# Placing the down-weight sums of a two-layer decoder trunk at single products instead of behind whole pairs

## The chip, the cores and the metric

The kernel runs on one core of a Trainium2 chip. A core has a matrix engine (PE in the profile, with its weight loads as PEld), a vector engine (DVE), a scalar engine (ACT), a general engine (POOL), a queue engine that only issues transfers (SP), and 16 DMA engines that all queues share. The metric is the device time of one execution in microseconds; times given for a kernel are medians of several runs.

## The reference

The reference is a decoder trunk of two layers on a sequence of 512 positions with 1024 channels, in 32-bit floats. Layer 0 mixes tokens by causal pooling, layer 1 by causal differential attention; each is followed by a dense SwiGLU block of 2816 hidden channels. Only that block is touched here:

```
x = layernorm(ALPHA * x + mixer(x))
x = layernorm(ALPHA * x + (silu(x @ w_gate) * (x @ w_up)) @ w_down)
```

## The kernel before

Every 32-bit operand is held as two parts, a rounded high part and a low remainder, and a product is three matmuls (high by high, high by low, low by high). ACT makes the high part (a cast) and DVE the low part (a subtraction). Weights come from one DRAM tensor, `wall`, in rows of 128x1024.

**The gate and up products.** The function `ffn(layer, late)` is called once per layer, as `ffn(0, ...)` and `ffn(1, ...)`. The 22 hidden blocks of 128 are taken two at a time as eleven units, 0 to 10, in the order `f0 f1 f2 p2 f3 p3 p4 p5 p6 p7 p8 p9 p10`: a unit `f` is half a pair made plainly, a unit `p` a whole pair made by a fast matrix scheme with seven products instead of eight. Pairs 4 to 10 make the seven in the order P1, Q5, P6, Q3, P7, P2, Q4 (`GATE`; `strassen(k)`). Each product needs a weight piece of its own, `g_N` with parts `g_Nh` and `g_Nl`; the pieces of pair 5 are g_29 to g_35, of pair 9 g_57 to g_63, of pair 10 g_64 to g_70, in the order of the products. P1, P6, P7 and Q4 add up in the PSUM bank A, Q5 and Q3 in the bank C, P2 in the bank B. Between products partial results are copied out: P1 from A to B by ACT (L1000), Q5 from C to `hid` by ACT (L1002), P6 from A to `hid` by ACT (L1004), Q3 and P7 by DVE (L1009, L1011). A product that adds to a bank must wait until the bank's last copy is done: so Q3 waits for L1002, P6 for L1000, P7 for L1004. `ahead(...)` has the pieces of the next products prepared up to six products ahead (L697 sums of weight rows on DVE, L700 casts on ACT, L703 remainders on DVE). The pieces go through six buffers in turn.

**The sums of down weights.** The product with `w_down` comes later (the down stage) and uses the same fast scheme, so it needs sums of blocks of `w_down`. They are made while the gate and up products run, in eleven steps, sum 0 to sum 10, in order:

- `load_terms(k)`: POOL issues two loads of four blocks (L808) and then one transfer that adds blocks to the first two (L809, an accumulating DMA that waits for the loads). For even k below 10 the place is a set of rows of `hid` that is not yet in use, for odd k and for 10 the tile `b`, of which there is one.
- `sum_terms(k)`, first half: two DVE additions of 128x512 (L814, L815). Second half: ACT issues two DMAs (L819) that write the four results to `tsum` in DRAM, and POOL issues `load_terms(k + 2)`. Since `load_terms(10)` reuses `b`, it is issued behind sum 9, and its loads wait until both writes of sum 9 have landed.

`weight_sums()` does the first half at once and leaves the second half to `catch_up()`, which is called behind the `ahead` of every product. So the writes of a sum stand one product behind its additions in ACT's order.

The program is written out by hand in this order, and each engine runs its own instructions in order. An instruction that waits holds what stands behind it on its engine, a DMA issue on ACT included. In the printed lists of an engine's rows the names read out<-in.

Of the kernel before, what the change touches and what calls it, by code (L numbers as in the profile page):

```python
# [49 lines left out]
EARLY = (1, 0)  # L50
PRE = SPLIT[:2]
SUMS = {1: (2, 1), 2: (2, 1)}
SUMMED = {"f0": 0, "p2": 0, "p4": 2, "p10": 0}
EAGER = 6


# [20 lines left out]
def trunk(ctx, tc, x, wall, pscale, lam_p, subln, table, lng, lnb, band, first, onehot, out):  # L77
# [6 lines left out]
    def bank(name):  # L84
        return ps.tile([P, 512], F32, tag="bank", name=name)
# [481 lines left out]
    def ffn(layer, late):  # L567
# [7 lines left out]
        with tc.tile_pool(name=f"ffn{layer}", bufs=1) as fp:  # L575
# [115 lines left out]
            def do_step(at=0):  # L691
                kind, j = steps.pop(at)
                c, pair = chunks[j]
                refill()
                t = raws[c]
                if kind == "sum":
                    tt(t, raws[pair[0]], raws[pair[1]], op=ALU.add)  # L697
                elif kind == "cast":
                    halves[j] = weight_pair(f"g{layer}_{j}")
                    nc.scalar.copy(halves[j][0], t)  # L700
                else:
                    h, l = halves[j]
                    tt(l, t, h.bitcast(F32), op=ALU.subtract)  # L703
                    finished.add(j)
                for d in set((c,) + pair):
                    if uses[d] == (kind, j):
                        raws.pop(d)
                        held[0] -= 1
# [103 lines left out]
            def sum_terms(k):  # L812
                t = terms.pop(k)
                tt(t[:, 1, 1], t[:, 0, 0], t[:, 1, 1], op=ALU.add)  # L814
                tt(t[:, 1, 0], t[:, 1, 1], t[:, 1, 0], op=ALU.add)  # L815
                yield
                dst = tsum[:, k // 2, :, term_slice(k)].rearrange("(j r) p t -> p j r t", j=2)
                for j in range(2):
                    nc.scalar.dma_start(out=dst[:, j], in_=t[:, j])  # L819
                if k + 2 < HALF - 1:  # L820
                    load_terms(k + 2)
                if k == HALF - 2:
                    load_terms(HALF - 1)
# [4 lines left out]
            def weight_sums():  # L828
                g = sum_terms(summed_rows[0])
                summed_rows[0] += 1  # L830
                next(g)
                behind.append(g)
# [4 lines left out]
            def catch_up():  # L837
                for g in list(behind):
                    if next(g, g) is g:
                        behind.remove(g)  # L840
# [49 lines left out]
            def both(t):  # L890
                return t.rearrange("p (f t) -> p f t", f=2)

            def half_product(acc, j, left, start, stop, high_first=False):
                h, l = halves[j]
                xh, xl = left
                terms_of = ((h, xh), (h, xl), (l, xh))
                places = [(f, kk) for f in range(2) for kk in range(4)]
                if high_first:
                    todo = [(f, kk, w, x) for w, x in terms_of for f, kk in places]
                else:  # L900
                    todo = [(f, kk, w, x) for f, kk in places for w, x in terms_of]
                for i, (f, kk, w, x) in enumerate(todo):
                    c = slice((4 * f + kk) * P, (4 * f + kk + 1) * P)
                    nc.tensor.matmul(  # L904
                        acc[:, f * 256 : (f + 1) * 256], w[:, c], x[:, kk, :],
                        start=start and i == 0,
                        stop=stop and i == len(todo) - 1,
                        skip_group_check=True,
                    )
# [70 lines left out]
            def strassen(k):  # L980
                names = {"P1": "A", "P6": "A", "P7": "A", "Q4": "A", "Q5": "C", "Q3": "C", "P2": "B"}
                begun = k in PRE
                banks = {"A": pre_a[k] if begun else bank(f"A{layer}_{k}"), "C": bank(f"C{layer}_{k}")}
                banks["B"] = bankB
                rows = hid[:, k : k + HALF + 1 : HALF, :]
                first, second = rows[:, :, :256], rows[:, :, 256:]

                def tile_of(i):
                    return keep.tile([P, S], F32, tag="y", name=f"sg{layer}_{k}_{i}", bufs=2)

                for p in BEGUN if begun else GATE:
                    acc = banks[names[p]]
                    j = number[k, GATE.index(p), "pair"]
                    half_product(
                        acc, j, lefts[p], p in ("P1", "Q5"), p in ("Q4", "Q3", "P2"),
                        k == PRE[0] and p == "Q4",
                    )
                    acc = both(acc)
                    if p == "P1":
                        nc.scalar.copy(both(bankB), acc)  # L1000
                    elif p == "Q5":
                        nc.scalar.copy(second, acc)  # L1002
                    elif p == "P6":
                        nc.scalar.copy(first, acc)  # L1004
                    elif p == "Q3":
                        if begun:
                            g0 = pre_g[k]
                            nc.scalar.activation(g0, g0, AF.Silu)
                        tt(first, acc, first, op=ALU.subtract)  # L1009
                    elif p == "P7":  # L1010
                        tt(second, second, acc, op=ALU.subtract)  # L1011
                    elif p == "P2":
                        g0 = tile_of(0)
                    else:
                        g1 = tile_of(1)
                        nc.scalar.activation(both(g1), acc, AF.Silu)  # L1016
                    if k == PRE[0] and p == "Q5":
                        while steps[0] != ("low", number[k, 6, "pair"]):
                            do_step()
                    else:  # L1020
                        ahead(j + lookahead(k, p))
                    if not (k == PRE[0] and p == "Q5"):
                        catch_up()
                    if p == "P2":
                        nc.scalar.activation(both(g0), acc, AF.Silu)
                    elif p == "Q4":
                        tt(first, both(g0), first, op=ALU.mult)  # L1027
                        tt(second, both(g1), second, op=ALU.mult)
                sum_hidden(k)

            for kind, i in units(layer):
                (plain if kind == "f" else strassen)(i)
                unit = f"{kind}{i}"
                for _ in range(SUMMED.get(unit, 1)):
                    weight_sums()
                if unit in AFFINE:
                    affine(n - 1, *AFFINE[unit])
# [634 lines left out]
```

## Time and profile before

| what | us |
|---|---|
| median of 3 runs (lowest, highest) | 934.05 (932.45, 934.33) |
| the profiled execution: its own time | 930.78 |
| the profiled execution: span from first to last instruction | 929.0 |
| PE busy in that span | 916.7 |
| DVE busy | 804.6 |
| ACT busy | 530.2 |
| POOL busy | 110.5 |

The granted clock of PE was 0.997 in the mean. Times inside the execution are microseconds from the start of the span. The gate and up stage of layer 0 with its pairs 4 to 10 lies at about 120 to 262, that of layer 1 at about 675 to 816. A row of a timeline reads: start, duration, engine, line, operation, out<-in, shape, count, and in brackets how long the engine sat idle just before it and what ended that. ACTq and POOLq are the sequencers of ACT and POOL. In the list of DMA issues the last number of a row is the time in microseconds from the issue to the landing.

### The profile page before, as it was taken

Reading aid. Unit: us, or ns where it says so; the run is one execution under the profiler, and the core shown is the slowest. Engines: PE = TensorE matmul, PEld = TensorE weight load, DVE = VectorE, ACT = ScalarE, POOL = GpSimd, SP = SyncE. Lnnn points to the kernel's source line nnn. Section 1 sums busy time; section 2 is a strip of 40 time slices with the busy share of each in tenths; the row PEclk is TensorE's granted clock in tenths of the full one; section 3 lists DMA queues with packets and bytes.
Section 4 is the critical chain, followed back from the end, with each engine's and each line's share of the span. In section 5 each row is a group of like instructions: output and inputs, shape, how many; then the busy total and the mean of one; then the engine's idle time right before and its main releaser. Section 6 shows DMA issues by size and latency. Waiting matters only on the chain. (4 is left out here: it accounts for less than half of the span.)

```text
span 929.0 us, 15065 instructions
## 1 busy us (share of the span) xinstructions
PE 916.7 (99%) x5806; PEld 826.2 (89%) x5806; DVE 804.6 (87%) x1163; ACT 530.2 (57%) x841; POOL 110.5 (12%) x129
## 2 busy tenths in 40 slices
PE   9999999999999999999999999999999999999996
PEld 8999899999988888888888888989999999988885
DVE  8997798999889997868989786877898998989988
ACT  6773354444555557776878864843454444655551
POOL 4121112110000001201111100201111110000001
PEclk9999999999999999999999999999999999999998
DMA  8497888985756578876665522467888985745563
GB/s 230 168 269 222 272 257 270 288 258 183 236 174 202 195 241 235 224 194 166 153 153 155 155 92 77 142 199 242 275 254 264 286 278 181 227 171 204 193 205 102
DMA packets 72518, 192.50 MB, mean 207 GB/s; under 512 B 14548, under 2 KB 14804, under 8 KB 72446
## 3 DMA queue, kind: packets, MB, share of 16 engines
q1 hardware_dynamic: 44572, 121.36, 39.1%
q0 software_dynamic: 15712, 46.93, 22.1%
q10 hardware_dynamic: 12162, 23.25, 6.7%
q8 instruction: 45, 0.74, 0.3%
q14 instruction: 27, 0.22, 0.1%
HBM read 166.33 MB, written 25.19 MB: 206 GB/s over the span
## 5 line engine op out<-in xcount | busy, mean ns | idle before, releaser
L697 DVE TENSOR_TENSOR raw<-raw,raw 128x1024 f32<-128x1024 f32 x72 | 87.8, 1221 | 6.8 <-DMA raw<-in_wall 5.8
L156 DVE TENSOR_TENSOR xs<-hid,xs 128x512 fp32r<-128x512 f32 x84 | 53.4, 637 | 0.0
L155 ACT CAST xs<-hid 128x512 fp32r<-128x512 f32 x84 | 48.5, 580 | 0.4 <-DVE hid L1027 0.4
L1303 ACT ACTIVATE p<-p,mn 128x128 f32<-128x128 f32 (+3 forms) x64 | 35.2, 552 | 14.1 <-DVE mn L1298 14.1
L808 POOL DMA_DIRECT2D b<-in_wall x24 | 18.9, 875 | 132.8 <-DMA tsum<-b 52.6
L1002 ACT COPY hid<-C 128x512 f32<-128x512 f32 x18 | 10.6, 588 | 33.9 <-PE C L904 16.0
L1298 DVE CUSTOM_DVE_ANT_0 p<-s,bias 128x128 f32<-128x128 f32 (+3 forms) x64 | 28.0, 485 | 1.1 <-PE s L1283 1.1
L808 POOL DMA_DIRECT2D hid<-in_wall x20 | 15.0, 753 | 112.3 <-DVE hid L814 35.8
L1009 DVE TENSOR_TENSOR hid<-C,hid 128x512 f32<-128x512 f32 x18 | 12.4, 689 | 16.5 <-PE C L904 13.2
L231 POOL TENSOR_TENSOR rs<-rs,mhalf 128x1 f32<-128x1 f32 x16 | 12.8, 802 | 103.2 <-DVE rs L230 96.2
L282 ACT ACTIVATE y<-pt,bT,gT 128x128 f32<-128x128 f32 x40 | 15.0, 456 | 15.9 <-PE pt L268 15.8
L1016 ACT ACTIVATE sg<-A 128x512 f32<-128x512 f32 x18 | 10.7, 596 | 22.7 <-PE A L904 22.7
L222 DVE BATCH_NORM_STATS2 st<-res 128x6 f32<-128x512 f32 x32 | 22.2, 694 | 1.1
L1004 ACT COPY hid<-A 128x512 f32<-128x512 f32 x18 | 10.6, 587 | 21.4 <-PE A L904 21.4
L809 POOL DMA_DIRECT2D b<-in_wall x12 | 14.8, 1230 | 60.5 <-DMA b<-in_wall 60.5
L1317 DVE SCALAR_TENSOR_TENSOR p<-p,sm,p 128x128 f32<-128x128 f32 (+3 forms) x32 | 17.6, 551 | 1.1
L1011 DVE TENSOR_TENSOR hid<-hid,A 128x512 f32<-128x512 f32 x18 | 12.3, 682 | 7.2 <-PE A L904 7.0
L762 ACT CAST xs<-hid 128x1024 fp32r<-128x1024 f32 x8 | 8.4, 1051 | 14.3 <-DVE hid L771 8.7
L261 DVE TENSOR_TENSOR res<-res,gb 128x512 f32<-128x512 f32 (+1 forms) x20 | 16.0, 799 | 0.7
L156 POOL TENSOR_TENSOR sql<-sq,sqh 128x512 fp32r<-128x512 f32 x7 | 9.3, 1324 | 60.5 <-ACT sqh L155 60.5
L260 DVE TENSOR_TENSOR res<-res,gb 128x512 f32<-128x512 f32 (+1 forms) x20 | 15.8, 792 | 0.0
L809 POOL DMA_DIRECT2D hid<-in_wall x10 | 12.4, 1241 | 28.7 <-DMA hid<-in_wall 28.6
(1218 smaller groups left out, 3561.7 us busy)
## 6 DMA issues: line engine op xcount, KB each, us to landing
raw<-in_wall SPq DMA_DIRECT2D x130, 512.0 KB, 5.7
r<-tsum SPq DMA_DIRECT2D x40, 512.0 KB, 3.7
b<-in_wall POOLq DMA_DIRECT2D x36, 512.0 KB, 6.1
hid<-in_wall POOLq DMA_DIRECT2D x30, 512.0 KB, 6.6
r<-in_wall SPq DMA_DIRECT2D x30, 512.0 KB, 4.1
tsum<-b ACTq DMA_DIRECT2D x24, 512.0 KB, 5.5
tsum<-hid ACTq DMA_DIRECT2D x20, 512.0 KB, 5.9
tall<-in_wall POOLq DMA_DIRECT2D x3, 1024.0 KB, 12.4
```

Of the source, the lines that this page charges most:

```text
L155: nc.scalar.copy(dst_h, src)
L156: (low or nc.vector).tensor_tensor(dst_l, src, dst_h.bitcast(F32), op=ALU.subtract)
L222: nc.vector.bn_stats(stats[n, s][:, d, :], res[:, s, d * 512 : (d + 1) * 512])
L260: nc.vector.tensor_tensor(z, z, gb[:, 0, c], op=ALU.mult)
L261: nc.vector.tensor_tensor(z, z, gb[:, 1, c], op=ALU.add)
L282: nc.scalar.activation(y[:, k, :], pt[:, k * P : (k + 1) * P], AF.Identity, bias=bT[:, n, kk : kk + 1], scale=gT[:, n, kk : kk + 1],)
L697: tt(t, raws[pair[0]], raws[pair[1]], op=ALU.add)
L808: nc.gpsimd.dma_start(out=t[:, j], in_=src[:, j])
L809: nc.gpsimd.dma_start(out=t[:, 0], in_=src[:, :, 1], accum_op=ALU.add)
L1298: nc.vector.tensor_tensor_reduce(out=p, in0=accs[c], in1=biases[h][:, w - 1 :: -1] if w < S else biases[h][:, ::-1], op0=ALU.add, op1=ALU. ...
L1303: nc.scalar.activation(p, p, AF.Exp, bias=mn[:, q, c : c + 1], scale=-1.0, accum_out=sm[:, q, c : c + 1],)
L1317: nc.vector.scalar_tensor_tensor(p0[:, r], p0[:, r], sm[:, q, 0:1], p1[:, r], op0=ALU.mult, op1=ALU.add)
```

## The change

`SUMMED` was a table that said how many sums are made behind a unit (one where nothing was said); it becomes a list of places. A place is the end of a unit, as before, or a product within a pair, behind the `catch_up()` of that product.

```diff
-SUMMED = {"f0": 0, "p2": 0, "p4": 2, "p10": 0}
+SUMMED = ("f1", "f2", "f3", "p3", "p4", "p5P2", "p6P7", "p7P7", "p8P6", "p9Q5", "p9")
...
                     if not (k == PRE[0] and p == "Q5"):
                         catch_up()
+                    if f"p{k}{p}" in SUMMED:
+                        weight_sums()
...
                 unit = f"{kind}{i}"
-                for _ in range(SUMMED.get(unit, 1)):
+                if unit in SUMMED:
                     weight_sums()
```

| sum | 0 | 1 | 2 | 3 | 4 | 5 | 6 | 7 | 8 | 9 | 10 |
|---|---|---|---|---|---|---|---|---|---|---|---|
| before: behind | f1 | f2 | f3 | p3 | p4 | p4 | p5 | p6 | p7 | p8 | p9 |
| now: behind | f1 | f2 | f3 | p3 | p4 | P2 of p5 | P7 of p6 | P7 of p7 | P6 of p8 | Q5 of p9 | p9 |

The instructions are the same in kind and number on every engine; the lines behind the second edit move down by two (L1025, L1027 and L1028 before are L1027, L1029 and L1030 now), the lines 697 to 1016 that are named here stay. Both layers change alike. Where the order moves, in layer 0:

ACT at the front of pair 5, before (the writes of sums 4 and 5, between the copies of P1 and Q5):

```order
L1000 COPY B_3_679<-A_5_1629 128x512 [waits PE_49,Activation_49]
L819 DMA tsum_539<-hid_537 128x2x512 [waits DMAHW3_49,DMASW6_49]
L819 DMA tsum_539<-hid_537 128x2x512 [waits DMAHW4_49,DMASW5_49,DVE_49]
L819 DMA tsum_539<-b_5_1429 128x2x512 [waits DMASW1_49]
L819 DMA tsum_539<-b_5_1429 128x2x512 [waits DMASW0_49,DVE_49]
L1002 COPY hid_537<-C_5_1630 128x2x256 [waits PE_49]
L700 CAST g_36h<-raw_1489 128x1024 [waits DMAHW0_49]
```

and now:

```order
L1000 COPY B_3_679<-A_5_1627 128x512 [waits PE_49,Activation_49]
L819 DMA tsum_539<-hid_537 128x2x512 [waits DMAHW3_49,DMASW6_49]
L819 DMA tsum_539<-hid_537 128x2x512 [waits DMAHW4_49,DMASW5_49,DVE_49]
L1002 COPY hid_537<-C_5_1628 128x2x256 [waits PE_49]
L700 CAST g_36h<-raw_1489 128x1024 [waits DMAHW0_49]
```

The copy L1002 of pair 5 no longer stands behind the writes of sum 5 (tile b_5).

ACT at the front of pair 9, before (the writes of sum 9, tile b_9):

```order
L1000 COPY B_3_679<-A_9_2555 128x512 [waits PE_49,Activation_49]
L819 DMA tsum_539<-b_9_2127 128x2x512 [waits DMAHW5_49,DMASW5_49]
L819 DMA tsum_539<-b_9_2127 128x2x512 [waits DMASW4_49,DVE_49]
L1002 COPY hid_537<-C_9_2556 128x2x256 [waits DMAHW7_49,DMAHW0_49,PE_49]
L700 CAST g_64h<-raw_2415 128x1024 [waits DMAHW2_49]
L1004 COPY hid_537<-A_9_2555 128x2x256 [waits PE_49]
L700 CAST g_65h<-raw_2415 128x1024 [waits DVE_49]
```

and now:

```order
L1000 COPY B_3_679<-A_9_2553 128x512 [waits PE_49,Activation_49]
L1002 COPY hid_537<-C_9_2554 128x2x256 [waits DMAHW2_49,DMAHW1_49,PE_49]
L700 CAST g_64h<-raw_2411 128x1024 [waits DMAHW0_49]
L1004 COPY hid_537<-A_9_2553 128x2x256 [waits PE_49]
L819 DMA tsum_539<-b_9_2281 128x2x512 [waits DMASW5_49]
L819 DMA tsum_539<-b_9_2281 128x2x512 [waits DMASW4_49,DVE_49]
L700 CAST g_65h<-raw_2411 128x1024 [waits DVE_49]
```

Both writes of sum 9 moved from behind P1's copy to behind P6's copy, two products later. At the front of pair 10 the writes of sum 10 keep their place between L1000 and L1002.

DVE from pair 8's end to Q3 of pair 9, before and now (sum 9 is the pair L814, L815):

```order
L835 TENSOR_TENSOR hid_537<-hid_537 128x256 [waits DVE_49]
L814 TENSOR_TENSOR b_9_2127<-b_9_2127 128x512 [waits DMAHW2_49,DMASW5_49,DMASW4_49]
L815 TENSOR_TENSOR b_9_2127<-b_9_2127 128x512 [waits DVE_49]
L260 TENSOR_TENSOR res<-res,gb_530 128x512
L261 TENSOR_TENSOR res<-res,gb_530 128x512 [waits DVE_49]
L703 TENSOR_TENSOR g_62l<-raw_2384,g_62h 128x1024 [waits PE_49,Activation_49]
L703 TENSOR_TENSOR g_63l<-raw_2187,g_63h 128x1024 [waits PE_49,Activation_49]
L703 TENSOR_TENSOR g_64l<-raw_2415,g_64h 128x1024 [waits DMAHW2_49,PE_49,Activation_49]
L1009 TENSOR_TENSOR hid_537<-C_9_2556,hid_537 128x2x256 [waits DMAHW0_49,DMAHW7_49,PE_49,Activation_49]
```

```order
L835 TENSOR_TENSOR hid_537<-hid_537 128x256 [waits DVE_49]
L260 TENSOR_TENSOR res<-res,gb_530 128x512
L261 TENSOR_TENSOR res<-res,gb_530 128x512 [waits DVE_49]
L703 TENSOR_TENSOR g_62l<-raw_2380,g_62h 128x1024 [waits PE_49,Activation_49]
L703 TENSOR_TENSOR g_63l<-raw_2179,g_63h 128x1024 [waits PE_49,Activation_49]
L814 TENSOR_TENSOR b_9_2281<-b_9_2281 128x512 [waits DMAHW3_49,DMAHW5_49,DMASW5_49,DMASW4_49]
L815 TENSOR_TENSOR b_9_2281<-b_9_2281 128x512 [waits DVE_49]
L703 TENSOR_TENSOR g_64l<-raw_2411,g_64h 128x1024 [waits DMAHW0_49,PE_49,Activation_49]
L1009 TENSOR_TENSOR hid_537<-C_9_2554,hid_537 128x2x256 [waits DMAHW1_49,DMAHW2_49,PE_49,Activation_49]
```

The additions of sum 9 moved behind four other instructions of DVE, ahead of g_64l.

## The prediction

> **What bounds the kernel now.** I read the page's first part, then the list of waits of PE, then the timelines of PE, ACT, DVE and POOL at the places that the change touches. The page and the two waits of PE that lie in the pairs:
>
> ```profile
> PE 916.7 (99%) x5806; PEld 826.2 (89%) x5806; DVE 804.6 (87%) x1163; ACT 530.2 (57%) x841; POOL 110.5 (12%) x129
> ...
> PE A L904 <- ACT hid L1004: 1.4, 1, 1.4
> PE C L904 <- ACT hid L1002: 1.0, 1, 1.0
> ```
>
> PE is busy for 916.7 of 929.0 us. The change touches no matmul, so it can only take away waits of PE or add some, and the list has two in the whole gate and up work. PE's timeline places them, and shows a smaller one in layer 1:
>
> ```profile
> 110.82 0.50 PE L904 MATMUL A<-xs,g_19h 128*128 128x256 f32 x2 [1.38 <-ACT hid L1004]
> ...
> 148.42 0.28 PE L904 MATMUL A<-xs,g_31l 128*128 128x256 f32 x1
> 149.67 0.39 PE L904 MATMUL C<-xs,g_32h 128*128 128x256 f32 x1 [0.97 <-ACT hid L1002]
> ...
> 703.76 0.28 PE L904 MATMUL A<-xs,g_31l 128*128 128x256 f32 x1
> 704.05 0.50 PE L904 MATMUL C<-xs,g_32h 128*128 128x256 f32 x2
> ```
>
> The first, at 110.82, is in pair 3, ahead of every sum that moves; it stays. The second is Q3 of pair 5. Elsewhere in these pairs the first matmul of a product follows the last one of the product before by 0.12 us, so Q3 could have started at 148.54 and came 1.13 us late; in layer 1 it could have started at 703.88 and came 0.17 late. From there to Q3 of pair 10 PE runs without a gap:
>
> ```profile
> 250.56 0.40 PE L904 MATMUL C<-xs,g_67h 128*128 128x256 f32 x2
> 804.95 0.40 PE L904 MATMUL C<-xs,g_67h 128*128 128x256 f32 x2
> ```
>
> These are 250.56 - 149.67 = 100.89 and 804.95 - 704.05 = 100.90 us for 35 products, 2.88 each (24 matmuls at 0.12). So 1.30 us is all that PE loses at the moved places.
>
> **What the change takes away.** Why Q3 of pair 5 is late, on DVE and ACT:
>
> ```profile
> 147.17 0.69 DVE L814 TENSOR_TENSOR b<-b 128x512 f32<-128x512 f32 x1 [1.36 <-DMA b<-in_wall]
> ...
> 145.85 0.37 ACTq L819 DMA_DIRECT2D tsum<-hid  x1
> 147.12 1.87 ACTq L819 DMA_DIRECT2D tsum<-b  x2
> 149.03 0.59 ACT L1002 COPY hid<-C 128x512 f32<-128x512 f32 x1 [4.59 <-PE A L904]
> ...
> 701.55 0.69 DVE L814 TENSOR_TENSOR b<-b 128x512 f32<-128x512 f32 x1 [0.93 <-DMA b<-in_wall]
> ```
>
> DVE wants to make sum 5 right behind sum 4, but its terms land only at 147.15. ACT has come to the writes of sum 5 and waits too; behind them stands L1002, behind that PE's Q3. From the landing of the terms to the start of Q3 it is 149.67 - 147.15 = 2.52 us, in layer 1 704.05 - 701.55 = 2.50: additions, issue of the second write, copy, release. This is a price that I use again below.
>
> With the change sum 5 is made after P2, five products later, so both its writes and DVE's wait leave this place. Sum 4's last write was issued at 145.85, so L1002 can run from about 146.2, and Q3 starts on time. Gain: 1.13 + 0.17 = 1.30 us. Its ends: 0, if something else were late there, and 1.30; I take 1.30, because the row at 145.85 shows what is next, and it is 2 us early.
>
> **What is moved and stays hidden.** Each sum is 1.4 us of DVE and two issues of 0.37 us on ACT, the same before and after. Sum 8, now ahead of Q3 of pair 8, and sum 9, ahead of Q3 of pair 9, fall just before DVE's wait for Q3 (1.65 us idle before L1009, row below), so they fill idle time. Sums 6 and 7 go behind P7, in the crowded half of a pair; rows of pair 8, which has the same rhythm:
>
> ```profile
> 221.79 1.23 DVE L697 TENSOR_TENSOR raw<-raw,raw 128x1024 f32<-128x1024 f32 x1
> ...
> 221.96 0.60 ACT L1016 ACTIVATE sg<-A 128x512 f32<-128x512 f32 x1 [0.96 <-PE A L904]
> 225.72 0.58 ACT L1000 COPY B<-A 128x512 f32<-128x512 f32 x1
> ...
> 227.52 0.40 PE L904 MATMUL A<-xs,g_59h 128*128 128x256 f32 x2
> ```
>
> There the sum would start at 221.79 and end at about 223.2; ACT holds the write until then, at 223.6 come L1025 and L1016 (0.6 each), two casts (1.05 each) and the copy L1000 (0.58), in all 3.9 us if nothing overlaps: 227.5. P6 needs L1000 at 227.52. It is hidden with next to nothing to spare; 0.5 us more would overlap in ACT's pipeline (L1016 and the cast behind it start 0.49 apart). Cost 0, with an upper end of 0.3 us at each of four places. The later loads of terms 7, 8 and 9 still have ten products of 2.88 us or more.
>
> **What the change adds: the load of terms 10.** These terms go into the one tile b, so their load waits for both writes of sum 9; sum 10 stays behind pair 9. Before:
>
> ```profile
> 226.46 0.69 DVE L815 TENSOR_TENSOR b<-b 128x512 f32<-128x512 f32 x1
> 229.53 1.22 DVE L703 TENSOR_TENSOR g_63l<-raw,g_63h 128x1024 fp32r<-128x1024 f32 x1
> 233.54 0.69 DVE L1009 TENSOR_TENSOR hid<-C,hid 128x512 f32<-128x512 f32 x1 [1.65 <-issue]
> 245.88 0.69 DVE L814 TENSOR_TENSOR b<-b 128x512 f32<-128x512 f32 x1
> ...
> 227.18 0.37 ACTq L819 DMA_DIRECT2D tsum<-b  x1
> 230.60 0.59 ACT L1004 COPY hid<-A 128x512 f32<-128x512 f32 x1 [1.34 <-PE A L904]
> 247.88 0.59 ACT L1002 COPY hid<-C 128x512 f32<-128x512 f32 x1 [1.42 <-PE C L904]
> 781.57 0.37 ACTq L819 DMA_DIRECT2D tsum<-b  x1
> ...
> 231.72 1.14 POOL L808 DMA_DIRECT2D b<-in_wall  x2 [29.48 <-DMA tsum<-b]
> 237.95 1.22 POOL L809 DMA_DIRECT2D b<-in_wall  x1 [5.08 <-DMA b<-in_wall]
> 786.71 1.12 POOL L808 DMA_DIRECT2D b<-in_wall  x2 [31.94 <-DVE g_64l L703]
> 791.56 1.23 POOL L809 DMA_DIRECT2D b<-in_wall  x1 [3.73 <-DMA b<-in_wall]
> ```
>
> The chain of layer 0: second write issued at 227.18, loads at 231.72, accumulating transfer at 237.95. The list of DMA issues, asked at each of those moments, gives the landings, in this order: the write at 227.18; the write at 781.57; a write at 147.1, issued into busier queues; the two writes of sum 3 at 127, issued 0.5 us apart; the accumulating transfer at 237.95; that at 791.56.
>
> ```profile
> tsum<-b ACTq DMA_DIRECT2D x1, 512.0 KB, 3.6
> tsum<-b ACTq DMA_DIRECT2D x1, 512.0 KB, 4.6
> tsum<-b ACTq DMA_DIRECT2D x1, 512.0 KB, 5.3
> tsum<-b ACTq DMA_DIRECT2D x2, 512.0 KB, 6.9
> b<-in_wall POOLq DMA_DIRECT2D x1, 512.0 KB, 5.7
> b<-in_wall POOLq DMA_DIRECT2D x1, 512.0 KB, 6.2
> ```
>
> So terms 10 landed at 237.95 + 5.7 = 243.65 and 791.56 + 6.2 = 797.76, two microseconds ahead of sum 10 (245.88). How late may they land? By the price of pair 5 (the same instructions in the same order) Q3 of pair 10 is held once the landing is later than 250.56 - 2.52 = 248.04, or 804.95 - 2.50 = 802.45. The chain may slip by 4.39 us in layer 0 and 4.69 in layer 1 at no cost to PE.
>
> How far it slips. On DVE, with sum 9 gone from the front, g_63l starts 1.33 us sooner, at 228.20, and sum 9 follows it: 229.34 to 230.75. On ACT the writes now stand behind L1004 (230.60): the first goes out at about 230.65, the second at 231.02. That is 231.02 - 227.18 = 3.84 us later, in layer 1 too. And the two writes now leave together, while before the first had a head start of 2.2 us: the landing is bounded by the single ones (3.6; 4.6 in layer 1) and by the pair at 127 (6.9). I take 5.3, the row at 147.1 and the middle. The slip is 3.84 + 5.3 - 3.6 = 5.54 in layer 0, and 3.84 + 5.3 - 4.6 = 4.54 in layer 1. PE loses 5.54 - 4.39 = 1.15 us at Q3 of pair 10 in layer 0, and nothing (0.15 to spare) in layer 1. DVE waits about 3.3 us for sum 10 (243.65 + 5.54 - 245.88):
>
> ```profile
> 242.00:262.00 20.00, 20.00 (x169) 20.00 (x168) 17.11 (x21) 10.81 (x15) 0.00 (x0) 1.00 0.73 241
> ```
>
> In that stretch DVE is busy for 17.1 of 20 us, so most of the wait falls into idle time, and the remainders behind it (g_69l, g_70l) are for P2 and Q4, two and three products behind Q3; I cost it at nothing more.
>
> **The sum.** -1.30 + 1.15 = -0.15 us. On the profiled execution, 930.78, that is 930.6; the median of the runs lies 3.3 above it, and I take the difference alone: 934.05 - 0.15 = 933.9.
>
> **The rivals.** A, *the slip is hidden*: the load of terms 10 lands in time in both layers, so the wait at pair 5 is simply gone: -1.30, 932.75. For it: in layer 0 it needs a write of at most 4.15 us, and single ones took 3.6 and 4.6. Against it: two writes at once. The Trainium skill, "DMA: Bandwidth & Descriptors", section "Anatomy of one DMA", gives about 2.0 us plus the bytes over 436 GB/s for a transfer that POOL issues: an estimate of 3.2 us for 512 KB, 4.4 for two together, so 12.0 for writes, loads and accumulation, and terms 10 would be there at 243. By that page rival A holds; this trace disagrees, with 5.7 and 6.2 us for one accumulating transfer.
>
> B, *the wait is larger at pair 10 than it was at pair 5*: slower. The writes take 6.9 us as at 127, and the loads as long as those of sum 5:
>
> ```profile
> 134.58 1.48 POOL L808 DMA_DIRECT2D b<-in_wall  x2 [12.16 <-DMA tsum<-b]
> ```
>
> From 134.58 to the landing at 147.15 is 12.6 us; those of terms 10 took 11.9 and 11.05. Then the slips are 7.8 and 7.7, PE loses 3.4 + 3.0 = 6.4, and the time is 934.05 - 1.3 + 6.4 = 939.2. It turns slower than before at slips that together exceed 4.39 + 4.69 + 1.30 = 10.4 us (I forecast 10.1), and measurably so at 12.3. Against it: the DMA engines stand at 0.73 there (the last but one number of the row of the stretch 242 to 262), with room left.
>
> C, *sums 6 and 7 hold ACT*: L1000 comes late and P6 waits, 0.3 us at four places: 1.2 more, 935.1. For it the arithmetic above, against it the pipelining.
>
> D, *the wait at pair 5 stays*: it needs another cause than sum 5's terms; the rows at 147.12 and 147.17 speak against it, so I give it next to nothing.
>
> **How the numbers follow.** The forecast (the wait moves from pair 5 to pair 10 at about its old size, between -1 and +1.8) gets 0.50, A 0.20, B beyond 1.9 us 0.20, C 0.08, D 0.02. A change of under 0.2% (1.9 us) is about what a measurement of this kernel cannot tell from none. Nothing in the trace offers a gain above 1.3 us, so faster takes only part of A, where other executions lose more at pair 5 than the profiled one, and the scatter of the median: 0.09. Slower is B and a little of C: 0.22. Same: 0.69. The range goes from A less the scatter of the runs (0.8 us), 931.9, to the middle of B, 937.3.
>
> **What would show it.** In the profile after: Q3 of pair 5 follows g_31l by 0.12 us in both layers; sum 9's second write at about 231 - 1.1 (all later times move with the gain); DVE waits some 3 us for DMA ahead of sum 10; Q3 of pair 10 comes about 1 us late in layer 0, released by L1002, and nearly on time in layer 1; P6 of pairs 7 and 8 stays at its 2.88 us rhythm. I would be wrong if terms 10 land later than 251 in layer 0, or if PE waits at a place not named here.

## The result: slower, and the loss is at the place that the prediction had put at one microsecond

The changed kernel takes 939.17 us (median of 22 runs, 931.88 to 942.94), the kernel before 932.47 beside it on the same chip (22 runs, 930.4 to 934.33). The ratio is 1.0066, with a 95% interval from 1.0054 to 1.0079: slower by 6.7 us. The prediction was 933.9 in a range from 931.9 to 937.3, so the time lies outside. As a difference the miss is larger still: the forecast took 934.05 for the kernel before, a median of 3 runs, and put the change at -0.15 us; it came out at +6.7. The profiled execution took 937.46 us (span 935.7), against 930.78 of before, so the two traces can be compared: they differ by 6.68.

The page of the profile after, first part, and the two rows of PE's list of waits that lie in the pairs (total, count, longest):

```profile
PE 919.4 (98%) x5806; PEld 828.7 (89%) x5806; DVE 804.2 (86%) x1163; ACT 529.7 (57%) x841; POOL 110.4 (12%) x129
```

```profile
PE C L904 <- ACT hid L1002: 5.6, 3, 5.0
PE A L904 <- ACT hid L1004: 0.8, 1, 0.8
```

PE has the same 5806 matmuls, but is busy for 919.4 us instead of 916.7: some of them ran slower. And the wait for L1002, one of 1.0 us before, is now one of 5.0. PE's timeline shows where, pair 5 and pair 10 of layer 0, then of layer 1:

```profile
148.56 0.28 PE L904 MATMUL A<-xs,g_31l 128*128 128x256 f32 x1
148.69 0.40 PE L904 MATMUL C<-xs,g_32h 128*128 128x256 f32 x2
...
249.37 0.28 PE L904 MATMUL A<-xs,g_66l 128*128 128x256 f32 x1
254.69 0.79 PE L904 MATMUL C<-xs,g_67h 128*128 128x256 f32 x2 [5.05 <-ACT hid L1002]
...
259.68 0.40 PE L904 MATMUL A<-xs,g_68h 128*128 128x256 f32 x2
...
709.89 0.28 PE L904 MATMUL A<-xs,g_31l 128*128 128x256 f32 x1
710.01 0.40 PE L904 MATMUL C<-xs,g_32h 128*128 128x256 f32 x2
...
810.69 0.28 PE L904 MATMUL A<-xs,g_66l 128*128 128x256 f32 x1
811.34 0.50 PE L904 MATMUL C<-xs,g_67h 128*128 128x256 f32 x2 [0.37 <-ACT hid L1002]
814.31 0.40 PE L904 MATMUL A<-xs,g_68h 128*128 128x256 f32 x2
```

Q3 of pair 5 (g_32) now follows g_31l by 0.12 to 0.13 us in both layers: the gain of 1.30 us is there. Q3 of pair 10 (g_67) comes 5.20 us late in layer 0 (254.69 less 249.37 and 0.12) and 0.53 late in layer 1. And in layer 0 it then takes 259.68 - 254.69 = 4.99 us instead of 2.88, which is 2.11 more; in layer 1 2.97. Together 5.20 + 2.11 + 0.53 + 0.09 - 1.30 = 6.6 us, close to the 6.68 by which the two executions differ. (The wait of pair 3 came out 0.6 us shorter in this execution than in that of before; something like 0.7 us elsewhere I did not place.)

The chain that ends at L1002, in the timelines of ACT, POOL and DVE (layer 0, then layer 1):

```profile
229.53 0.89 ACTq L819 DMA_DIRECT2D tsum<-b  x2
229.99 0.43 ACTq L819 DMA_DIRECT2D tsum<-b  x1
254.05 0.59 ACT L1002 COPY hid<-C 128x512 f32<-128x512 f32 x1 [8.67 <-DVE b L815]
791.38 0.37 ACTq L819 DMA_DIRECT2D tsum<-b  x1
...
238.20 1.14 POOL L808 DMA_DIRECT2D b<-in_wall  x2 [26.13 <-DVE hid L1011]
242.34 1.22 POOL L809 DMA_DIRECT2D b<-in_wall  x1 [2.99 <-DMA b<-in_wall]
798.43 1.12 POOL L808 DMA_DIRECT2D b<-in_wall  x2 [24.86 <-DVE g_65l L703]
802.50 1.23 POOL L809 DMA_DIRECT2D b<-in_wall  x1 [2.95 <-DMA b<-in_wall]
...
252.19 0.69 DVE L814 TENSOR_TENSOR b<-b 128x512 f32<-128x512 f32 x1 [7.30 <-DMA b<-in_wall]
808.85 0.69 DVE L814 TENSOR_TENSOR b<-b 128x512 f32<-128x512 f32 x1 [2.63 <-DMA b<-in_wall]
```

The second row is the second write alone, at 229.99; in layer 1 it left at 791.38 (fourth row). The landings, in the list of DMA issues: the writes of sum 9 and the accumulating transfer of terms 10, in layer 0, then in layer 1:

```profile
tsum<-b ACTq DMA_DIRECT2D x2, 512.0 KB, 6.4
b<-in_wall POOLq DMA_DIRECT2D x1, 512.0 KB, 9.8
...
tsum<-b ACTq DMA_DIRECT2D x2, 512.0 KB, 5.6
b<-in_wall POOLq DMA_DIRECT2D x1, 512.0 KB, 6.3
```

The landings of the writes, 6.4 and 5.6, are those of the first of the two; that of the second is not in the trace, so the table below goes by the issue of the loads that wait for it. DVE sat idle for 7.3 us for terms 10, and ACT's L1002 stood behind it. The row that stands out is the 9.8: the same transfer took 5.7 us before.

**The slip, term by term.** Times of after less those of before; up to pair 9 the execution after ran 1.08 us ahead in layer 0 and 5.86 behind in layer 1 (DVE's L1009 of pair 9), which is taken out of the first row.

| from ... to | layer 0, predicted | layer 0, measured | layer 1, predicted | layer 1, measured |
|---|---|---|---|---|
| second write of sum 9 issued later by | 3.84 | 3.89 | 3.84 | 3.95 |
| second write to loads (L808) | +1.7 | 8.21 - 4.54 = +3.67 | +0.7 | 7.05 - 5.14 = +1.91 |
| loads to accumulating transfer (L809) | 0 | 4.14 - 6.23 = -2.09 | 0 | 4.07 - 4.85 = -0.78 |
| accumulating transfer to its landing | 0 | 9.8 - 5.7 = +4.1 | 0 | 6.3 - 6.2 = +0.1 |
| slip | 5.54 | 9.57 | 4.54 | 5.18 |
| less the slack of 4.39 or 4.69: PE waits | 1.15 | 5.2 | 0 | 0.5 |

So in layer 0 the two middle rows miss in opposite directions and nearly cancel (3.67 less the 1.7 predicted is 1.97, against -2.09); the accumulating transfer is the miss.

**The slow product.** The same stretch in the table of stages of after (the last three numbers are the granted clock, the DMA share and GB/s):

```profile
242.00:247.00 5.00, 5.00 (x44) 5.00 (x43) 2.86 (x5) 2.11 (x3) 1.22 (x1) 1.00 0.90 248
...
250.00:255.00 5.00, 0.31 (x1) 0.31 (x2) 2.74 (x5) 0.95 (x2) 0.00 (x0) 0.75 0.39 144
255.00:258.00 3.00, 3.00 (x15) 3.00 (x15) 3.00 (x3) 3.00 (x5) 0.00 (x0) 0.50 0.53 173
258.00:262.00 4.00, 4.00 (x31) 4.00 (x30) 3.07 (x5) 1.62 (x3) 0.00 (x0) 0.84 0.82 285
262.00:266.00 4.00, 4.00 (x35) 4.00 (x35) 3.55 (x5) 1.88 (x3) 0.00 (x0) 1.00 0.52 152
```

In the three microseconds behind the wait PE is busy all the time with 15 matmuls at a granted clock of 0.50; the first row has 44 in five microseconds, which is 26 in three, at 1.00.

### The profile page after: what moved, and what is told of

It reads as the page before. It is cut to its first block, busy times and chain, and to the rows that moved or that the text cites. A ratio compares the mean times of both kernels' runs of the same rounds, so it can differ in the third digit from the quotient of the medians.

```text
span 935.7 us, 15045 instructions
## 1 busy us (share of the span) xinstructions
PE 919.4 (98%) x5806; PEld 828.7 (89%) x5806; DVE 804.2 (86%) x1163; ACT 529.7 (57%) x841; POOL 110.4 (12%) x129
## 5 line engine op out<-in xcount | busy, mean ns | idle before, releaser
L808 POOL DMA_DIRECT2D b<-in_wall x24 | 17.9, 793 | 148.1 <-DMA tsum<-b 39.4
L1009 DVE TENSOR_TENSOR hid<-C,hid 128x512 f32<-128x512 f32 x18 | 12.4, 690 | 19.9 <-PE C L904 16.9
L1002 ACT COPY hid<-C 128x512 f32<-128x512 f32 x18 | 10.6, 587 | 32.6 <-PE C L904 14.5
L808 POOL DMA_DIRECT2D hid<-in_wall x20 | 15.0, 752 | 116.5 <-DVE hid L814 36.4
L1004 ACT COPY hid<-A 128x512 f32<-128x512 f32 x18 | 10.6, 587 | 21.3 <-PE A L904 21.3
L809 POOL DMA_DIRECT2D b<-in_wall x12 | 14.8, 1230 | 54.6 <-DMA b<-in_wall 54.6
L1027 ACT ACTIVATE sg<-B 128x512 f32<-128x512 f32 x14 | 8.3, 594 | 15.3 <-DVE b L815 6.2
L814 DVE TENSOR_TENSOR b<-b 128x512 f32<-128x512 f32 x12 | 8.2, 686 | 9.9 <-DMA b<-in_wall 9.9
L261 DVE TENSOR_TENSOR res<-res,gb 128x512 f32<-128x512 f32 (+1 forms) x20 | 16.0, 799 | 0.7
```

Source lines behind the costliest of these rows:

```text
L261: nc.vector.tensor_tensor(z, z, gb[:, 1, c], op=ALU.add)
L808: nc.gpsimd.dma_start(out=t[:, j], in_=src[:, j])
L809: nc.gpsimd.dma_start(out=t[:, 0], in_=src[:, :, 1], accum_op=ALU.add)
```

## The experiments

Each kernel is timed against the kernel before on the same chip, in three groups whose medians of before are 932.62, 932.18 and 932.21 us.

### Which part of the change loses

**Sum 9 put back behind pair 8**, all else as changed:

```diff
-SUMMED = ("f1", "f2", "f3", "p3", "p4", "p5P2", "p6P7", "p7P7", "p8P6", "p9Q5", "p9")
+SUMMED = ("f1", "f2", "f3", "p3", "p4", "p5P2", "p6P7", "p7P7", "p8P6", "p8", "p9")
```

> The changed kernel with sum 9 alone put back behind pair 8; sums 5 to 8 stay at their products. Theory T (all of the loss comes from terms 10 landing late because sum 9 moved; the rest of the change only takes the wait at pair 5 away): 1.3 us below before, 931.2 us on the 22 runs' 932.5, with PE's Q3 of pair 10 on time in both layers. Rival C (sums 6, 7 and 8 within their pairs hold ACT and cost time): stays well above before, up to 939.

Measured: 931.36 us (11 runs, 928.81 to 933.38), ratio 0.9988 (0.9976 to 1.0000), that is 1.26 us less than before. PE's list of waits has no L1002 left. All of the loss hangs on sum 9, and sums 6, 7 and 8 inside their pairs cost nothing that can be seen within the interval (about 1 us to each side).

**Only sum 9 moved**, the kernel before otherwise:

```diff
-SUMMED = {"f0": 0, "p2": 0, "p4": 2, "p10": 0}
+SUMMED = {"f0": 0, "p2": 0, "p4": 2, "p8": 0, "p10": 0}
...
+                    if (k, p) == (9, "Q5"):
+                        weight_sums()
```

> The kernel before with sum 9 alone moved behind Q5 of pair 9; all other sums stay behind their pairs. Theory T: the loss of the change without its gain, 932.5 + 6.7 + 1.3 = 940.5 us, with Q3 of pair 10 late. Rival C: no loss, 932.5. In between would say that the crowding of the earlier loads has a share in how late terms 10 are.

Measured: 937.86 us (8 runs, 932.79 to 940.52), ratio 1.0057 (1.0037 to 1.0078): 5.2 us more than before. So most of the loss comes with sum 9 alone, but not the 8.0 us that were expected of it. In its trace Q3 of pair 10 comes 2.96 us late in layer 0 and then takes 4.33 us; in layer 1 it is 0.19 late. The wait is 2.2 us shorter than in the changed kernel because the transfers were faster: the loads came 7.63 us behind the second write (8.21 there), and the accumulating transfer took 8.2 us (9.8); whether the other moved sums have a share in that, no run here tells. And the wait at Q3 of pair 5 is not in this trace, though sum 5 stands where it stood before: Q3 begins at 152.00, 0.12 us behind g_31l, and at 710.94 in layer 1, 0.12 behind as well. So the 1.30 us of the kernel before are not lost in every execution. The three microseconds behind the wait of layer 0 in its table of stages:

```profile
256.00:259.00 3.00, 3.00 (x19) 3.00 (x19) 3.00 (x4) 3.00 (x5) 0.00 (x0) 0.66 0.57 180
```

The granted clock is 0.66.

**Only sum 5 moved** to P2 of pair 5, sums 6 to 9 behind pairs 5 to 8 as before:

```diff
+SUMMED = ("f1", "f2", "f3", "p3", "p4", "p5P2", "p5", "p6", "p7", "p8", "p9")
```

> The kernel before with sum 5 alone moved behind P2 of pair 5; sums 6 to 10 stay behind their pairs. By the prediction's first term: 1.3 us below before (931.2), Q3 of pair 5 on time in both layers. If other executions lose more at pair 5 than the profiled one did, up to 3 us below. If the wait there had another cause, 932.5.

Measured: 931.34 us (11 runs, 930.13 to 933.2), ratio 0.9993 (0.9983 to 1.0004). The median is 1.28 less than that of before, against a predicted 1.30; the interval of the ratio still holds 1. The wait at Q3 of pair 5 is gone from the trace (which the trace above shows to happen without this edit too, so the medians carry more of the gain than this row).

**Sum 10 made later**, behind Q5 of pair 10, with sum 9 where the change has it:

```diff
+SUMMED = ("f1", "f2", "f3", "p3", "p4", "p5P2", "p6P7", "p7P7", "p8P6", "p9Q5", "p10Q5")
```

> The changed kernel with sum 10 made behind Q5 of pair 10 and not behind pair 9; sum 9 stays behind Q5 of pair 9, so terms 10 land as late as in the changed kernel. Theory T in its full form (the late landing costs only through DVE's and ACT's wait for it ahead of Q3 of pair 10): the wait is gone, since sum 10 is wanted two products (5.8 us) later and its writes stand behind P6's copy, one product more: 931.2 to 933 us. If the late transfers cost in another way (they meet the loads of the down stage), it stays near 939.

Measured: 931.29 us (11 runs, 929.39 to 932.46), ratio 0.9986 (0.9971 to 1.0000). Terms 10 are late here too, though less so: the accumulating transfer, issued at 243.74, took 8.3 us, and they landed at about 252.0, that is 0.6 us behind the start of Q3 of pair 10 (251.43), where in the changed kernel they landed 2.7 us behind the time at which Q3 was due. By the price of 2.5 us from landing to Q3 they would have held Q3 for 3.1 us, had sum 10 stayed behind pair 9. DVE still waits for them:

```profile
252.01 0.69 DVE L814 TENSOR_TENSOR b<-b 128x512 f32<-128x512 f32 x1 [1.58 <-DMA b<-in_wall]
```

but now L1002 stands ahead of the writes of sum 10 on ACT, and Q3 of pair 10 starts at once. So a late transfer costs PE nothing by itself; it cost because the copy that PE needs stood behind it.

### How the cost grows with the place of sum 9

```diff
-"p9Q5"
+"p9P1"      (first kernel)
+"p9P6"      (second kernel)
```

> The changed kernel with sum 9 behind P1 of pair 9, one product (2.9 us) sooner. By slip alone terms 10 land about 2.9 us sooner; of the changed kernel's 5.2 us wait in the profiled execution some 2 stay, without the slow clock behind it: about 933 us. If the landing is set by meetings with the loads of the down stage and not by the issue, it stays at 937 or more.

> The changed kernel with sum 9 behind P6 of pair 9, one product later. Each microsecond of slip is a microsecond of wait once the 4.4 us of room are used up: 2.9 us more in each layer, and a slow clock behind the wait in both layers (about 2 us each): 939.2 + 5.8 + 1 to 3 = 946 to 948 us. If landing is set by something else than the issue, it stays near 939.

Measured: behind P1 931.36 us (12 runs, 929.78 to 933.74), ratio 0.9987 (0.9975 to 0.9999); behind P6 945.5 us (5 runs, 944.34 to 947.8), ratio 1.0139 (1.0119 to 1.0159). With the two known places, in order: behind pair 8 931.36, P1 931.36, Q5 939.17, P6 945.5. One product earlier than the change there is no loss at all, one product later both layers wait, by 5.60 and 5.56 us, and both have the slow product behind it (5.28 and 5.29 us). In layer 0:

```profile
256.38 0.80 PE L904 MATMUL C<-xs,g_67h 128*128 128x256 f32 x2 [5.43 <-ACT hid L1002]
261.66 0.46 PE L904 MATMUL A<-xs,g_68h 128*128 128x256 f32 x2
```

The time of the second kernel is close to the 946 to 948 expected, but not in the way expected: the wait was to grow by 2.9 us in each layer, and it grew by 0.4 in layer 0 and by 5.0 in layer 1. The slips (the landing of terms 10 against the time at which Q3 of pair 10 was due, less the same in before) are 1.3 and 1.9 us behind P1, 9.6 and 5.2 behind Q5, 9.9 and 10.2 behind P6, for steps of 2.88 us: what the transfers meet counts as much as when they start. So the cost has an edge: nothing until the slack is used up, and then the wait and the slow product together.

### Why the accumulating transfer took 9.8 us

Two theories. G: the writes of sum 9 leave together and so land late. M: the accumulating transfer meets the loads of down weights (`r`, 512 KB each) that SP issues at this time. SP's rows in the timeline of after, layer 0:

```profile
239.58 0.33 SPq L609 DMA_DIRECT2D r<-in_wall  x1
243.29 0.33 SPq L609 DMA_DIRECT2D r<-in_wall  x1
```

One was issued 2.76 us ahead of the accumulating transfer, the next 0.95 us behind it. Before, the first of these came 2.70 us behind the transfer:

```profile
240.65 0.33 SPq L609 DMA_DIRECT2D r<-in_wall  x1
```

**The first write of sum 9 issued one product earlier than the second** (for G):

```diff
+                if k == HALF - 2:
+                    nc.scalar.dma_start(out=dst[:, 0], in_=t[:, 0])
                 yield
...
-                for j in range(2):
+                for j in range(k == HALF - 2, 2):
```

> The changed kernel, with the first of sum 9's two writes (its blocks need no addition) issued in ACT's order ahead of P6's copy and not behind it, about 2.4 us sooner; the second write and the additions stay. Theory G (the two writes leave together and so land 2 to 3 us later than apart): the landing of the second write falls back to 4 to 5 us from its issue, terms 10 land 2 us sooner, and the time falls by some 2 to 4 us to about 936. Rival P (the landing is late by position alone, 3.8 us, and by what the loads of terms 10 meet there): no change, 939.

Measured: 933.55 us (12 runs, 930.63 to 936.82), ratio 1.0012 (0.9998 to 1.0027), 5.6 us less than the changed kernel. But the trace gives another reason than G in layer 0. Rows of ACT and POOL, and from the list of DMA issues the landing of the transfer issued at 244.34:

```profile
229.42 0.37 ACTq L818 DMA_DIRECT2D tsum<-b  x1
232.41 0.37 ACTq L821 DMA_DIRECT2D tsum<-b  x1
...
240.25 1.15 POOL L808 DMA_DIRECT2D b<-in_wall  x2 [25.48 <-DVE hid L1013]
244.34 1.22 POOL L809 DMA_DIRECT2D b<-in_wall  x1 [2.94 <-DMA b<-in_wall]
```

```profile
b<-in_wall POOLq DMA_DIRECT2D x1, 512.0 KB, 6.2
```

From the second write to the loads it is 7.84 us, against 8.21 in after: G gives 0.4 us there. (In layer 1 it is 793.73 - 788.63 = 5.10 against 7.05, which G would explain, but little was at stake there.) What changed in layer 0 is the accumulating transfer, 6.2 instead of 9.8, though nothing was done to it but a shift in time against SP's loads, which now came 2.05 us ahead and 1.66 behind. So the time spoke for G, and the rows for M.

The kernel with sum 9 behind P6 speaks against G as well. In layer 0 its two writes left together too, 0.41 us apart, and yet the loads followed 4.73 us behind the second, which was issued at 237.36 (4.41 in layer 1):

```profile
236.96 0.89 ACTq L819 DMA_DIRECT2D tsum<-b  x2
242.09 1.15 POOL L808 DMA_DIRECT2D b<-in_wall  x2 [28.53 <-issue]
```

The nearest loads of SP were 7.7 us ahead of the second write and 3.5 behind it. In after two of them, of 512 KB each, were issued 2.75 us (a `raw` load, at 227.24) and 1.61 us ahead of it:

```profile
228.38 0.33 SPq L609 DMA_DIRECT2D r<-in_wall  x1
```

So leaving together is not enough to make the writes slow, and SP's loads are the likelier cause there too; no run left out these two loads, so this is not shown.

**The loads r_1 and r_2 left out** (for M; the first products of the down stage use other data):

```diff
+                if j in (1, 2):
+                    drops[j] = gbs[n - 1][:, 0, :]
+                    return
```

> The changed kernel without the loads of the second and third weight items of the down stage (r_1, r_2; SP issues them at 239.6 and 243.3 in the changed kernel); other data in the SBUF takes their place, so the first product of the down stage is made from wrong weights. Theory M (the accumulating transfer of terms 10 takes 9.8 us and not 5.7 because it meets these loads): it takes 5 to 6 us, PE's wait at pair 10 falls below 2 us, and the time is 932 to 934. Rival P (position alone): 939.

Measured: 937.44 us (6 runs, 936.15 to 940.4), ratio 1.0047 (1.0029 to 1.0066). The experiment did not do what it was made for: SP went on to r_3 and r_4 and issued them at the same place, 3.40 us ahead of the accumulating transfer and 0.31 behind it, and this took 9.7 us. It neither speaks for nor against M.

**The loads r_1 to r_4 issued, but cut to 16 columns**, 8 KB each:

```diff
+                if 1 <= j <= 4:
+                    nc.sync.dma_start(out=t[:, :16], in_=source(j)[:, :16])
+                    drops[j] = gbs[n - 1][:, 0, :]
+                    return
```

> The changed kernel, with SP's loads of items 1 to 4 of each down stage (r_1 to r_4, 512 KB each) cut down to 16 columns; the products of pass 1 of the down stage so use weights that were not loaded, and the output differs. Theory M (POOL's accumulating transfer of terms 10 is slow because it meets SP's loads): it lands in 5.5 to 6.5 us after its issue in layer 0 instead of 9.8, the wait at Q3 of pair 10 there falls from 5.2 us to between 1 and 2.5, the slow clock behind it goes for the most part, and the time is 933 to 936. Rival, that SP's loads do not matter to it: the transfer still takes 9 us or more, the wait stays at 5 to 6, the time at 937 to 940.

Measured: 932.51 us (12 runs, 930.7 to 934.53), ratio 1.0002 (0.9989 to 1.0016), 6.7 less than the changed kernel. SP's loads came 2.33 us ahead and 1.18 behind, nearly as in after. In layer 0, the loads and the accumulating transfer on POOL and then PE (the kernel's lines stand four lower here, so L1002 is L1006), and the landing of the transfer:

```profile
239.24 1.14 POOL L812 DMA_DIRECT2D b<-in_wall  x2 [25.70 <-DVE hid L1015]
243.58 1.22 POOL L813 DMA_DIRECT2D b<-in_wall  x1 [3.19 <-DMA b<-in_wall]
...
251.04 0.28 PE L908 MATMUL A<-xs,g_66l 128*128 128x256 f32 x1
252.29 0.51 PE L908 MATMUL C<-xs,g_67h 128*128 128x256 f32 x2 [0.97 <-ACT hid L1006]
```

```profile
b<-in_wall POOLq DMA_DIRECT2D x1, 512.0 KB, 6.2
```

The two writes still left together (231.21 and 231.67, 7.6 us ahead of the loads), the sum is where the change puts it, and the transfer lands in 6.2 us: the wait falls from 5.20 to 1.13 us, and Q3 takes 2.98. The time is a little below the 933 to 936 expected; what the smaller loads save elsewhere is not separated. M is shown for layer 0: without the bytes of SP's loads at that moment the 9.8 is a 6.2 (and with whole loads at nearly the same distances, 2.48 ahead and 1.24 behind, it is the 9.1 of the kernel with PE kept busy, below).

All 26 accumulating transfers of terms 10 in the thirteen traces, by what SP issued near them (us ahead and behind):

| SP's 512 KB loads near it | kernel and layer: us from issue to landing |
|---|---|
| 2.2 to 3.4 ahead and 0.3 to 1.5 behind | after 0: 9.8; r_1 and r_2 left out 0: 9.7; PE kept busy 0: 9.1; sum 10 later 0: 8.3; only sum 9 0: 8.2 |
| the same, but 8 KB | r_1 to r_4 cut 0: 6.2 (its layer 1, 1.6 ahead and 2.4 behind: 5.7) |
| none within 6 ahead, 0.2 behind | write apart 1: 7.8 |
| none within 6 ahead, 1.3 to 1.7 behind | four: 5.8 to 6.5 |
| 1.5 to 2.1 ahead, 1.7 to 2.2 behind | six: 6.0 to 7.0 (after 1: 6.3) |
| 3.0 and more ahead or none, 2.1 and more behind or none | eight, both of before among them: 5.7 to 6.7 |

The five slow ones are those that an SP load followed within 1.5 us while another was still under way; with 2.05 ahead and 1.66 behind (write apart 0) it is 6.2 again. Where both loads were whole they stood 3.7 us apart, so the table cannot tell which of the two distances counts. That a few tenths decide it is what the table shows; why they do, no run here tells.

### What the clock costs behind a wait

In layer 0, 44 matmuls that nobody reads, put into the wait:

```diff
+                    if (layer, k, p) == (0, HALF - 1, "Q3"):
+                        spin = bank("spin")
+                        for _ in range(44):
+                            nc.tensor.matmul(spin[:, :256], halves[j][0][:, :P], lefts[p][0][:, 0, :], ...)
```

> The changed kernel, in layer 0 alone, with 44 matmuls of 128x256 whose result nobody reads (by 0.12 us each 5.3 us) put on PE ahead of Q3 of pair 10, that is into the wait of 5.2 us. Theory, that about 2 us of the loss are the lower clock behind the wait: Q3 of pair 10 of layer 0 takes 2.9 to 3.1 us instead of 4.99, nothing else changes, and the time is 936.5 to 938 (about 2 us under the changed kernel's 939.2), though the wait is now paid as work. Rival, that the slow matmuls behind the wait have another cause (their operands arriving late, contention with the copies): Q3 still takes 4 to 5 us, and the time is 939 to 940.

Measured: 939.13 us (6 runs, 936.72 to 943.6), ratio 1.0084 (1.0062 to 1.0106). The time did not fall. PE's rows and the stage behind the wait say why:

```profile
251.69 5.44 PE L997 MATMUL spin<-xs,g_67h 128*128 128x256 f32 x44
256.96 0.40 PE L904 MATMUL C<-xs,g_67h 128*128 128x256 f32 x2
259.85 0.40 PE L904 MATMUL A<-xs,g_68h 128*128 128x256 f32 x2
...
255.21 0.59 ACT L1009 COPY hid<-C 128x512 f32<-128x512 f32 x1 [7.63 <-DVE b L815]
```

```profile
255.00:258.00 3.00, 3.00 (x27) 3.00 (x26) 2.96 (x4) 2.79 (x5) 0.00 (x0) 1.00 0.67 255
```

With PE kept busy the clock stays at 1.00 and Q3 takes 2.89 us: that part came as expected, and shows that the slow product is the wait's own second cost. But the spare matmuls took as long as the wait that they replace (251.69 to 256.96, 5.27 us against 5.20), while the wait would have been shorter in this execution: the copy that Q3 needs (here L1009) began at 255.21 and took 0.59, so they ran 1.1 us too long. From the time at which Q3 was due to its end layer 0 took 8.16 us here and 10.19 in the changed kernel, so 2.0 us were won; layer 1 waited 1.37 us, against 0.53, and lost 0.8. The 1.2 us that are left do not show in the medians. The times decide nothing; the clock and the length of Q3 do.

The waits at Q3 of pair 10 in all kernels, from 0.5 us on, with the length of the product behind each: 0.53 then 2.97, 0.77 then 2.98, 0.84 then 2.98, 1.13 then 2.98, 1.37 then 2.98; 2.96 then 4.33; 5.20 then 4.99, 5.56 then 5.29, 5.60 then 5.28, 5.72 then 5.26. Waits up to 1.4 us leave 0.1 behind, waits from 3 us on leave 1.45 to 2.4.

Between the two the traces have the wait of pair 3 in layer 0 (the one for L1004, 1.5 us in the trace of before), and there it is not the length alone that decides. In nine of the thirteen traces it was 1.9 to 2.5 us; in six of these the product behind it took 4.2 to 4.5 us, in the other three 3.06, the same as behind the shorter waits there. Two waits of the same 2.03 us, with PE kept busy and with sum 10 later, in three microseconds that begin 1.0 us behind the end of the wait:

```profile
112.70:115.70 3.00, 3.00 (x16) 3.00 (x16) 2.09 (x3) 0.59 (x1) 0.00 (x0) 0.50 1.03 409
113.90:116.90 3.00, 3.00 (x25) 2.87 (x25) 2.84 (x5) 0.59 (x1) 0.00 (x0) 1.00 1.02 407
```

The first brought the half clock, the second did not. So some executions of one kernel can pay 1.1 to 1.4 us there that others do not. The Trainium skill, "TensorE: Matmul & The Clock Gate", section "Part 1: The HAM clock gate", says that the clock falls to half after an idle window of about 3.4 us, that the window runs freely, and that full speed comes back after about as long a busy time. The half clock and a window that runs freely agree with the rows above (0.50 at 255 to 258; the 0.84 of 258 to 262 puts its end at about 259.3, 4.6 us behind the start of Q3; the same 2.03 us with and without it). The idle window of 3.4 us does not: a wait of 2.96 us was followed by a clock of 0.66 in the three microseconds behind it, and one of 2.03 us by 0.50; there the measurement decides.

### A version that beats both

Sum 9 behind P1 and sum 10 behind Q5, both free in earlier runs, and the pieces prepared one product later at one place of unit f3, right ahead of pair 3, so that the silu and the copy of P6 no longer stand behind two casts on ACT:

```diff
-SUMMED = (..., "p8P6", "p9Q5", "p9")
+SUMMED = (..., "p8P6", "p9P1", "p10Q5")
...
-                    ahead(j + i + (6 if (f, i) == (3, 1) else 5))
+                    ahead(j + i + 5)
```

> The changed kernel with sum 9 behind P1 of pair 9 and sum 10 behind Q5 of pair 10 (neither made PE wait in earlier runs), sum 3 in its first form place (f3), and casts put one product later at one place of pair 3, so that ACT's silu and copy there no longer stand behind two casts. If the 1.4 to 2 us that PE waits at P7 of pair 3 in layer 0 come from those two casts, they go, and the time is 929.3 to 930.2 against 931.4 of the kernel with sum 9 behind P1 alone. Rival, that the wait there follows from something earlier on DVE (the casts are late whatever stands ahead): the wait stays, and the time is 931 to 932; if the moved casts come too late for their own products, 932 or more.

Measured: 929.92 us (11 runs, 929.27 to 930.71), ratio 0.9978 (0.9969 to 0.9986), 2.3 us less than before and 9.3 less than the changed kernel. PE's waits in the pairs, of this kernel:

```profile
PE C L904 <- ACT hid L1002: 0.9, 2, 0.6
```

The wait for L1004 in pair 3 (1.4 us before) is gone, and a shorter one for L1002 stands a product later. The kernel with sum 9 behind P1 alone was at 931.36, so the medians differ by 1.4 us, as expected; the intervals of the two ratios overlap and two places differ, so the row of the wait carries more of this than the times. The eleven runs lie within 1.4 us of each other, those of before beside them within 7.0: a wait that brings a slow product in some executions only would scatter the times in this way, though no run separates it.

## Why the prediction was wrong, step by step

- **The gain of 1.30 us at pair 5: right.** Both rows show Q3 on time, and the four kernels that have the gain without the loss lie 0.8 to 1.3 us under before, with intervals of the ratio that end between 0.9999 and 1.0004. It is a gain of some executions: with sum 9 alone moved the wait was not there to be taken away.
- **Sums 6, 7 and 8 inside the pairs at nothing: right.** Rival C, which priced them at 1.2 us, falls with the kernel that has sum 9 put back (931.36), within about 1 us.
- **The second write later by 3.84 us: right** (3.89 and 3.95). The slack, and the 2.5 us from landing to Q3, also held: 242.34 + 9.8 = 252.14, and Q3 began 2.55 us later.
- **The slip in layer 0: this is the step that failed.** It let only the landing of the writes change, by 1.7 us, and carried the loads and the accumulating transfer over with the durations they had before. The writes cost 3.67, of which the shorter loads gave 2.09 back, but the accumulating transfer took 9.8 us instead of 5.7. So PE waited 5.20 us at Q3 of pair 10 where 1.15 was forecast. The transfer's time was read from a place where no SP load was issued for 2.70 us behind it; the change moved it past one and up to the next. The loads of SP are not in the prediction's working at all, though the change shifts the whole chain against them; the run that cut them down brought the transfer back to 6.2 and the wait to 1.13. The prediction put the slower writes down to their leaving together, which the kernel with sum 9 behind P6 does not bear out (0.41 us apart, loads 4.7 and 4.4 us later). The argument against rival B, a DMA share of 0.73 over twenty microseconds, was an average: in after the share is 0.90 from 242 to 247 and 0.39 from 250 to 255, and what counted was the moment.
- **The wait at its own length: too low by 2.11 us.** The prediction costed a wait at its length alone, in its own 1.15 and in the 6.4 of rival B. The product behind the wait of 5.20 us ran at half the clock for the most part and took 2.11 us more.
- **Layer 1: right in kind.** Predicted 0 with 0.15 us to spare, measured 0.53: the writes there took 1.9 us more than before, where 0.7 was predicted, and the loads 0.8 less.
- **The rivals.** The outcome lies where B was (slower, with the wait at pair 10 larger than the one at pair 5, to 939.2), with other terms: B had the writes and loads longer in both layers, at 3.4 + 3.0 us; it was 5.2 + 2.1 in one layer and 0.6 in the other, so that B's 939.2 meets the measured 939.17 by chance, and from 934.05 instead of 932.47 at that. A did not happen, nor the 3.2 us per transfer that was worked out beside it (for ACT's writes too, though the figure is for transfers that POOL issues): the accumulating transfers took 5.7 to 9.8. The range cut B in its middle (between B's ends, 934.05 + 1.9 and 939.2, that is 937.6, not 937.3), with a chance of 0.20; the terms that could only make a slip larger deserved more than that.

## What to carry to other kernels

When a chain of transfers is moved in time, list what every other queue issues beside its new place; durations read at the old place need not hold there (one grew by 4.1 us here, another shrank by 2.1), and a share of the DMA engines averaged over twenty microseconds does not show the collision. Before a wait on a shared tile is moved, look at what stands behind the waiting instruction: sum 10 two products later cost nothing, though its terms still came too late for the old place. And a wait of PE that reaches some 3 us is to be priced with the slow product behind it, here 1.5 to 2.4 us more; from some 2 us on such a product came in six of nine cases.

## What was not expected of the hardware

- The same accumulating transfer of 512 KB took 5.7 to 7.0 us in twenty cases (in two of them beside loads cut to 8 KB), 7.8 in one, and 8.2 to 9.8 in the five where SP's next load came within 1.5 us behind it with another under way.
- Behind two writes of 512 KB issued 0.4 to 0.5 us apart, the loads that wait for them came 7.0 to 8.8 us after the second write where SP had issued two loads within 2.8 us ahead of it (twelve cases), and 4.7 and 4.4 us after it where SP's nearest was 7.7 us ahead. Behind writes issued 1.9 to 3.4 us apart it was 4.4 to 6.0, with one at 7.8.
- A wait of 2.96 us, not only one of 5, brought the granted clock down, to 0.66 over three microseconds; one of 2.03 us brought it down to 0.50 in one trace and left it at 1.00 in another.
